# Compression of the cached keys in a hybrid decoder step: three float32r products per weight slice, two row tiles to a PSUM bank in one chunk, and one operand loaded earlier

## The chip, the cores and the metric

The program runs on one core of one Trainium2 chip. The metric is the device time of one launch in microseconds (us), taken as the median over runs. The profiled execution is a separate run with its own time.

## The reference, cut to what matters

One inference step of a two-layer decoder trunk: 512 prompt tokens and 8 sequences of 8 sample tokens. Each layer projects its input with one matrix `w_in` (columns for a convolution, for a sparse attention with compressed, selected and windowed branches, and for a differential attention), mixes, and runs a SwiGLU block. The change touches the compression of keys and values, which runs for "k" and for "v" in each layer, over the 1024 cached positions of 8 sequences and over the 512 prompt positions:

```
def nsa_compress(k, pe, w1, b1, w2):
    B, L, G, D = k.shape
    n16 = L // CMP_STRIDE
    k16 = k[:, :n16 * CMP_STRIDE].reshape(B, n16, CMP_STRIDE, G, D)
    blk = jnp.concatenate([k16[:, :-1], k16[:, 1:]], axis=2) + pe[None, None, :, None, :]
    blk = blk.transpose(0, 1, 3, 2, 4).reshape(B, n16 - 1, G, CMP_LEN * D)
    return jax.nn.gelu(blk @ w1 + b1) @ w2
```

CMP_STRIDE is 16, D is 64, G is 2, so one compressed column is a product over 2048 numbers (16 slices of 128), and neighbouring columns overlap by half.

## The kernel before

One layer runs in stages. `merge` interleaves two generators in program order: `projections` (weight WP) and `compressions` (weight WC); then `prompts` and `samples` (the two attentions); then the output projection with a norm, and the feed-forward block. The tile framework reorders instructions on each engine by its own timeline, so what stands in a queue is read from the built program. Each engine works its queue in order. Loads and stores go through SyncE's queue (SP), gathers of cache pages through GpSimd's (POOL).

**Splitting.** Nearly all dense products are made of float32r halves: `split` writes h = round(x) with ScalarE and l = x - h with VectorE, and `product` adds three matmuls, h·wh, h·wl and l·wh. The 64 sample rows hold h and l side by side in one tile, so for them two matmuls do.

**Chunks.** `chunk` computes 128-token row tiles m = 0..3 and the sample tile m = 4 of a range of columns of `w_in` with `dense_tok`. Its weights stream in eight slices kt. The order of the chunks is d (512 columns), c (280), q (512), e (256); between q and e stand `sample_queries` and `diff_operands`. Five accumulators take the PSUM tags a0, a0, a1, a1, t0. Tag t0 has one buffer, a0, a1 and t1 have two each, h has one. The sinks of the q tiles transpose through t0 as well (line 649, eight groups of four).

**Compression.** `compress` goes over five blocks p: four of two cached sequences, 256 columns (both groups), and one of the prompt, 64 columns. `gather` or `load` brings a page in; `cmp_keys` transposes it through t1 (line 757), and four copies of 64 partitions per bank (line 747 and after, helper line 217) put it into two tiles `kt`. Then 16 plain float32 matmuls with N + 1 columns run over it:

```
for k in range(16):
    aa, jp = k // 4, k % 4
    mm(hid[:, :N + 1], w1[k], kt[jp // 2][:, jp % 2, aa:aa + 2 * N + 1:2], k == 0, k == 15)
```

Their moving columns are every second column of `kt`; the odd last one carries the position embedding. `hid` has the tag h.

**sample_queries** takes an H slot, loads the selection matrix `selp` from the constants, and multiplies it with the gates of the sample rows (`t<-gates,H` in the profile).

Tiles of tags U (30 slots of 1152 words) and H (26 slots of 512 words) are handed out by `W`, the slot freed longest ago first, and returned by `free`; a load into a slot waits for that slot's last reader. Helper lines: 181 load, 184 store, 187 `act`, 190 `tt`, 216 and 217 `cp` (VectorE, ScalarE), 227 `mm`, 350 the transposes of x.

Of the kernel before, what the change touches and what calls it, by code (L numbers as in the profile page):

```python
# [9 lines left out]
F = mybir.dt.float32  # L10
# [38 lines left out]
WC = 120.0  # L49
# [86 lines left out]
def kernel(ctx: ExitStack, tc: tile.TileContext, a: dict, o: dict, nlayers: int = DEPTH):  # L136
# [225 lines left out]
    def product(out, s_, wh, wl, first, last):  # L362


        if not isinstance(s_, tuple):
            mm(out, s_, wh, first, False)
            mm(out, s_, wl, False, last)
        else:
            hs, ls = s_
            mm(out, hs, wh, first, False)  # L370
            mm(out, hs, wl, False, False)
            mm(out, ls, wh, False, last)

    def dense_tok(w_rows, KT, N, st, sink, tail=0, last="h", done=None, raws=None, nh=8):


        acc = [PS(b) for b in ("a0", "a0", "a1", "a1", last)]
# [10 lines left out]
        def step(kt, m, wh, wl):  # L388
            first, last = kt == 0, kt == KT - 1
            out = acc[m][:, :N]  # L390
            product(out, st(kt, m), wh, wl, first, last)
# [20 lines left out]
        for m in (4, 0, 1, 2, 3) if last == "t0" else range(5):  # L412
            for kt, wh, wl, _ in res:
                step(kt, m, wh, wl)
            sink(m, acc[m])
# [39 lines left out]
    def layer(l, x, x_src, raws):  # L455
# [102 lines left out]
        def chunk(c0, N, sink, raws=None):  # L558
            def evac(m, acc):
                z = W("H", [128 if m < 4 else NS, N])  # L560
                if m < 4:
                    cp(z, acc[:, :N])
# [127 lines left out]
        def attention_columns():  # L690
            for c in ORDER:
                if c == "c":
                    new_kv("win")
                if c == "e":
# [25 lines left out]
        def cmp_weights(which):  # L720
            w1s = [W("U", [128, 8, 128]) for _ in range(2)]
            for i in range(2):
                load(w1s[i], a["cmp_w1_" + which][l, i * 1024:(i + 1) * 1024].rearrange("(k p) n -> p k n", p=128))
            w1 = [w1s[k // 8][:, k % 8] for k in range(16)]
# [10 lines left out]
            peT = T("cpe" + which, [128, 2, 2, 4])  # L735
            V.tensor_copy(peT, pt[:, :16].rearrange("p (a q i) -> p q i a", q=2, i=2))
# [3 lines left out]
        def cmp_keys(which, peT, p):  # L740


            n = 128 if p < 4 else 64
            slots = 4 if p < 4 else 2
            kt = [W("U", [128, 2, slots * n + 4]) for _ in range(2)]
            for q in range(2):
                V.tensor_copy(kt[q][:, :, slots * n:], peT[:, q])
            for b2 in range(2 if p < 4 else 1):
                if p < 4:
                    nat = gather("cache_nsa_cmp_" + which, l, 2 * p + b2)  # L750
                else:
                    nat = W("U", [64, 8, 128])
                    load(nat, o["p_cmp_" + which][l, 0].rearrange("(p j) g d -> p j (g d)", j=8))
                for q in range(2):
                    pt = PS("t1").rearrange("p (k t) -> p k t", k=4)
# [879 lines left out]
```

## Time and profile before

| what | value |
|---|---|
| median of 3 runs | 2069.74 us (2063.65 to 2074.16) |
| profiled execution, its own time | 2071.4 us |
| its span (first to last instruction) | 2069.6 us |
| busy share PE / PE weight loads / DVE / ACT / POOL | 93% / 79% / 53% / 44% / 10% |
| mean granted TensorE clock | 0.969 of full speed |

A matmul's duration in the profile includes the time in which it overlaps its neighbours; what a run of matmuls costs is read from start to start. A plain float32 matmul shows as two records of the same shape, a float32r matmul or a float32 transpose as one. The clock column gives 1.00 for 2.4 GHz and 0.50 for 1.2 GHz.

### The profile page before, as it was taken

The numbers are of one execution on the slowest core, as the hardware profiler recorded it, in microseconds if no ns is written. First come the engines' busy times: TensorE is split into PE (matmuls) and PEld (weight loads), VectorE is DVE, ScalarE is ACT, GpSimd is POOL, SyncE is SP. The second block draws the span as 40 slices with busy tenths as digits, with TensorE's granted clock in tenths as the row PEclk, the third lists the DMA queues.
The fourth block names the chain that finished last, engine by engine and source line by source line (L and its number), as shares of the span: only waits on it lengthen the run. The fifth ranks groups of instructions, "written<-read, shape, count | busy, mean of one in ns | idle before, by whom it ended". The sixth has DMA issues, their size and how long they took to land. (4 is left out here: it accounts for less than half of the span.)

```text
span 2069.6 us, 32882 instructions
## 1 busy us (share of the span) xinstructions
PE 1933.5 (93%) x12222; PEld 1631.7 (79%) x12222; DVE 1101.2 (53%) x3012; ACT 916.7 (44%) x2368; POOL 206.7 (10%) x233
## 2 busy tenths in 40 slices
PE   8999888989999999999999997989899999999997
PEld 6887765656689999988879776656566899999885
DVE  3568476866573333323456665678666633333236
ACT  3635565767422333321245545667673223333211
POOL 2011022121010000000120110221110000000002
PEclk9999899999999999999999998999999999999999
DMA  6423143243423332352153321441433332324411
GB/s 200 137 76 103 28 145 128 83 146 99 136 92 117 97 122 83 93 187 77 48 174 108 96 71 45 152 155 57 138 108 118 112 122 82 122 84 130 149 56 51
DMA packets 190252, 223.91 MB, mean 108 GB/s; under 512 B 19092, under 2 KB 138812, under 8 KB 189948
## 3 DMA queue, kind: packets, MB, share of 16 engines
q1 hardware_dynamic: 171660, 154.69, 24.5%
q0 software_dynamic: 18432, 67.12, 10.2%
q8 instruction: 97, 1.59, 0.3%
q14 instruction: 63, 0.52, 0.1%
HBM read 206.23 MB, written 24.15 MB: 111 GB/s over the span
## 5 line engine op out<-in xcount | busy, mean ns | idle before, releaser
L227 PE MATMUL a<-H,U 128*128 128x512 f32 (+3 forms) x2264 | 552.8, 411 | 14.0 <-ACT H L187 11.6
L190 DVE TENSOR_TENSOR H<-H,H 128x512 fp32r<-128x512 f32 (+5 forms) x392 | 255.5, 657 | 510.5 <-ACT H L187 482.8
L227 PEld LDWEIGHTS a<-H,U 128*128 128x128 f32 (+1 forms) x2264 | 386.2, 190 | 111.2 <-issue 15.4
L187 ACT ACTIVATE H<-H 128x512 fp32r<-128x512 f32 (+4 forms) x418 | 240.8, 583 | 519.9 <-DMA H<-in_ffn_w_dram 298.8
L227 PE MATMUL a<-U,H 128*128 128x288 f32 (+2 forms) x3008 | 399.2, 306 | 7.9 <-DMA U<-in_cache_diff_v_dram,idx 6.7
L227 PEld LDWEIGHTS a<-U,H 128*128 128x128 f32 (+1 forms) x3008 | 370.2, 181 | 21.7 <-DMA U<-in_cache_diff_v_dram,idx 7.3
L227 PE MATMUL t<-U,H 128*128 128x288 f32 x1584 | 288.7, 297 | 0.4 <-ACT U L187 0.4
L227 PEld LDWEIGHTS t<-U,H 128*128 128x128 f32 x1584 | 243.5, 190 | 1.0 <-ACT U L187 0.6
L227 PE MATMUL a<-U,U 128*128 128x512 f32 (+4 forms) x744 | 200.7, 379 | 7.9 <-ACT H L187 3.7
L227 PE MATMUL h<-U,U 128*128 128x257 f32 (+5 forms) x708 | 152.4, 376 | 13.1 <-ACT U L217 13.0
L217 ACT ACTIVATE U<-t 64x256 f32<-64x256 f32 (+4 forms) x393 | 142.8, 366 | 45.6 <-PE t L757 24.5
L227 PEld LDWEIGHTS a<-U,U 128*128 128x128 f32 x744 | 129.4, 191 | 34.2 <-ACT U L187 7.4
L227 PEld LDWEIGHTS h<-U,U 128*128 128x128 f32 (+1 forms) x708 | 114.6, 185 | 40.3 <-ACT U L217 17.3
L227 PE MATMUL h<-U,H 128*128 128x288 f32 x528 | 140.9, 296 | 0.0
L187 ACT ACTIVATE U<-H 128x288 fp32r<-128x288 f32 (+4 forms) x160 | 64.4, 438 | 143.8 <-DVE H L190 104.1
L217 ACT ACTIVATE H<-t 128x512 f32<-128x512 f32 (+1 forms) x172 | 94.9, 564 | 45.6 <-PE t L1145 23.5
L547 DVE SCALAR_TENSOR_TENSOR U<-U,cw,U 128x512 f32<-128x512 f32 x240 | 109.4, 510 | 0.1
L227 PEld LDWEIGHTS h<-U,H 128*128 128x128 f32 x528 | 99.3, 188 | 0.0
L190 POOL TENSOR_TENSOR U<-U,U 128x512 f32<-128x512 f32 x24 | 33.6, 1417 | 599.1 <-DVE rs_u L321 459.9
L187 ACT ACTIVATE U<-t 128x256 fp32r<-128x256 f32 (+4 forms) x132 | 47.1, 370 | 97.0 <-PE t L350 40.8
L190 DVE TENSOR_TENSOR U<-H,U 128x64 fp32r<-128x64 f32 (+6 forms) x204 | 69.9, 385 | 31.1 <-ACT U L187 24.8
L216 DVE COPY H<-t 128x512 f32<-128x512 f32 (+1 forms) x92 | 57.2, 626 | 45.7 <-PE t L1214 15.6
(293 smaller groups left out, 2268.9 us busy)
## 6 DMA issues: line engine op xcount, KB each, us to landing
H<-in_ffn_w_dram SPq DMA_DIRECT2D x264, 256.0 KB
H<-in_w_in_dram SPq DMA_DIRECT2D x64, 256.0 KB
H<-in_w_out_dram SPq DMA_DIRECT2D x32, 256.0 KB
xd<-U SPq DMA_DIRECT2D x24, 256.0 KB
U<-xd SPq DMA_DIRECT2D x12, 512.0 KB
U<-in_x_prompt_dram SPq DMA_DIRECT2D x8, 512.0 KB
H<-in_state_nsa_win_v_dram SPq DMA_DIRECT2D x16, 256.0 KB
H<-in_state_nsa_win_k_dram SPq DMA_DIRECT2D x16, 256.0 KB
```

Source lines behind the costliest of these rows:

```text
L187: S.activation(out, in_, func, **kw)
L190: return (eng or V).tensor_tensor(out, x, y, op=op)
L216: return V.tensor_copy(out, in_)
L217: return S.activation(out, in_, AF.Copy)
L227: return PE.matmul(out, lhsT, rhs, start=start, stop=stop)
L547: V.scalar_tensor_tensor(out=ac, in0=ex, scalar=wc, in1=ac, op0=OP.mult, op1=OP.add)
```

## The change

In the compression, `cmp_weights` splits w1 into wh and wl (two U tiles each), and the position embedding into halves as well. `compress` first copies a page with ScalarE into two H tiles `halves` (four copies of 256 elements per partition), which puts the two groups side by side, and frees the page. `cmp_keys` then works for one half q: it transposes four 128-wide pieces, and one `split` per bank writes the h and l tiles of `kt` with rows of equal parity (r) contiguous. The 16 slices, now eight per half q, have three float32r matmuls each on contiguous columns: 256 of them (258 in the first block, 64 in the prompt's). The embedding's columns, two VectorE copies per block before, come by four small GpSimd copies per block.

In `dense_tok`, a chunk with 2N <= 512 (only chunk e, N = 256) puts two row tiles into one bank: a0, a0 and a1 in place of five banks; the first matmul of the second tile of a bank waits for that of the first one, and the copy out waits for both tiles.

`selp` is loaded before chunk q, not in `sample_queries`. WC goes from 120 to 128.

```diff
-        acc = [PS(b) for b in ("a0", "a0", "a1", "a1", last)]
+        if 2 * N > 512:
+            acc = [PS(b) for b in ("a0", "a0", "a1", "a1", last)]
+        else:
+            acc = [t[:, c * 256:(c + 1) * 256] for t in (PS(b) for b in ("a0", "a0", "a1")) for c in range(2)]
...
+                if c == "q":
+                    own["selp"] = W("H", [64, 512])
+                    load(own["selp"], a["cst"][:64, CST["selp"][0]:CST["selp"][0] + 512])
...
+                raw = W("U", [128, 8, 128])
+                load(raw, a["cmp_w1_" + which][l, i * 1024:(i + 1) * 1024].rearrange("(k p) n -> p k n", p=128))
+                wh, wl = (W("U", [128, 8, 128], FR) for _ in range(2))
+                split(wh, wl, raw)
...
-                for q in range(2):
-                    pt = PS("t1").rearrange("p (k t) -> p k t", k=4)
-                    for j in range(4):
-                        PE.transpose(pt[:, j, :n], nat[:, 4 * q + j], ident[:n, :n])
-                    for g in range(2):
-                        c0 = (b2 * 2 + g) * n
-                        for par in range(2):
-                            cp(kt[q][par * 64:(par + 1) * 64, :, c0:c0 + n], pt[g * 64:(g + 1) * 64, par::2, :n])
...
+            kt = [W("U", [128, 2, 2, len(nats) * n + 3], FR) for _ in range(2)]
+            for part in range(2):
+                G.tensor_copy(kt[part][:, :, :, len(nats) * n:], peT[:, part, q].bitcast(F))
+            for b2, nat in enumerate(nats):
+                pt = PS("t1")
+                for i in range(4):
+                    PE.transpose(pt[:, i * n:(i + 1) * n], nat[q][:, i * 128:(i + 1) * 128], ident[:n, :n])
+                split(*(t[:, :, :, b2 * n:(b2 + 1) * n] for t in kt), pt[:, :2 * w].rearrange("p (i c r) -> p i r c", i=2, r=2))
...
+                    for q in range(2):
+                        for g in range(2):
+                            act(halves[q][:, :, g], nat[:, 4 * q:4 * q + 4, g * 64:(g + 1) * 64].rearrange("p (i k) d -> p i k d", k=2))
...
+                            mm(hid[:, :M], wh, kh, first, False)
+                            mm(hid[:, :M], wh, kl, False, False)
+                            mm(hid[:, :M], wl, kh, False, last)
```

**The first block on PE.** The names are out<-moving,stationary; h is the accumulator, U tiles are `kt` and w1, first holds the identity, a and t with U and H are the chunk. Layer 0, block p = 0 of "k", before and then now:

```order
L227 MATMUL a_70_257<-H_111_482,U_31_125 128x512
L227 MATMUL a_70_257<-U_114_488,U_27_121 128x512
L227 MATMUL h_375<-U_87_331,U_76_279 128x257 x2
L757 MATMUL t_109_464<-first_63,U_108_462 128x128
L227 MATMUL h_375<-U_88_332,U_76_279 128x257 x2
```

```order
L227 MATMUL t_73_260<-H_109_451,U_32_126 128x512
L781 MATMUL t_106_424<-first_63,H_91_328 128x128 x4
L227 MATMUL h_359<-U_98_360,U_77_281 128x258
L227 MATMUL h_359<-U_99_361,U_77_281 128x258
L227 MATMUL h_359<-U_98_360,U_78_282 128x258
```

Each slice has three matmuls where it had one, and the transposes read copies in H tiles, not the gathered page.

**PE behind chunk q.** Layer 0; a with U_27 is the tail of chunk q, 128x256 is chunk e, lines 649 and 668 are the transposes of the q tiles, 1068, 1078, 1110 and 1120 those of `sample_queries`, 866 (910 now) those of `diff_operands`. Before and then now:

```order
L227 MATMUL a_378_2046<-U_421_2295,U_31_125 128x512
L227 MATMUL t_461_2474<-c_242_1310,H_410_2251 64x64 x4
L649 MATMUL t_437_2344<-first_63,H_434_2337 128x128 x4
L227 MATMUL t_464_2483<-gates_237,H_465_2484 128x24 x4
L1068 MATMUL t_467_2498<-first_63,H_424_2307 128x64 x4
L649 MATMUL t_438_2353<-first_63,H_429_2331 128x128 x4
L1068 MATMUL t_468_2507<-first_63,H_425_2308 128x64 x4
L1078 MATMUL t_469_2516<-first_63,H_268_1449 128x64 x4
L649 MATMUL t_443_2379<-first_63,H_440_2372 128x128 x4
L227 MATMUL t_470_2527<-c_242_1310,H_459_2467 32x64 x2
L227 MATMUL a_479_2566<-H_484_2571,U_24_118 128x256
```

```order
L227 MATMUL a_451_2501<-U_491_2755,U_31_125 128x512
L227 MATMUL t_530_2912<-gates_237,H_447_2496 128x24 x4
L668 MATMUL t_506_2799<-first_63,H_503_2792 128x128 x4
L227 MATMUL a_543_2986<-H_546_2989,U_24_118 128x256
L227 MATMUL a_544_2987<-H_546_2989,U_24_118 128x256
L227 MATMUL a_545_2988<-H_546_2989,U_32_126 128x256
L1110 MATMUL t_532_2925<-first_63,H_494_2767 128x64 x4
L1110 MATMUL t_533_2934<-first_63,H_495_2768 128x64 x4
L1120 MATMUL t_534_2943<-first_63,H_315_1739 128x64 x4
L227 MATMUL a_543_2986<-H_547_2990,U_24_118 128x256
```

The last products of the compression (`c` tiles) have left this place for one ahead of q's end, chunk e begins two entries behind the gates, and its sample tile goes to an a bank with the first slice, where it was the last to run in t0.

**SP around chunk e's loads.** in_cst with 64x512 is `selp`, in_w_in with 128x256 are slices of chunk e, cbv and c are vectors and weights of the next layer's compression. Before, then the two pieces of now:

```order
L181 DMA H_409_2233<-in_w_in_dram 128x512
L181 DMA H_495_2633<-in_w_in_dram 128x256
L181 DMA cbv_11966<-in_cmp_b_v_dram 128x1
L181 DMA H_465_2484<-in_cst_dram 64x512
L181 DMA H_486_2573<-in_w_in_dram 128x256
L181 DMA H_489_2593<-in_w_in_dram 128x256
L181 DMA H_504_2693<-in_w_in_dram 128x256
L181 DMA c_2229_10927<-in_cmp_w_k_dram 128x64 x2
L181 DMA H_506_2698<-in_w_in_dram 128x256
```

```order
L184 DMA out_p_win_v_dram<-H_431_2398 128x128
L181 DMA H_447_2496<-in_cst_dram 64x512
L184 DMA out_p_win_k_dram<-H_415_2307 128x128
L184 DMA out_s_win_k_dram<-H_403_2267 8x8x128
L184 DMA out_p_win_v_dram<-H_437_2441 128x128
L184 DMA out_p_win_k_dram<-H_426_2357 128x128
L181 DMA H_477_2658<-in_w_in_dram 128x512
```

```order
L181 DMA H_483_2704<-in_w_in_dram 128x512
L181 DMA cbv_12512<-in_cmp_b_v_dram 128x1
L181 DMA c_2295_11353<-in_cmp_w_k_dram 128x64 x2
L181 DMA H_548_2991<-in_w_in_dram 128x256
L181 DMA H_551_3011<-in_w_in_dram 128x256
L181 DMA H_563_3091<-in_w_in_dram 128x256
```

`selp` now stands ahead of all slices of chunk q, and chunk e's slices still stand behind the two loads for the next layer.

## Rows read from the trace of the kernel before

**Rows 1.** The page, busy time and share of the span.

```profile
PE 1933.5 (93%) x12222; PEld 1631.7 (79%) x12222; DVE 1101.2 (53%) x3012; ACT 916.7 (44%) x2368; POOL 206.7 (10%) x233
```

**Rows 2.** Windows: length, busy us of PE, PEld, DVE, ACT, POOL, clock, DMA.

```profile
40.00:240.00 200.00, 190.95 (x1081) 163.35 (x1080) 120.60 (x332) 103.40 (x278) 26.09 (x27) 0.99 0.32 92
240.00:282.00 42.00, 31.87 (x195) 29.09 (x196) 23.01 (x63) 21.14 (x58) 3.87 (x5) 0.72 0.28 74
...
1264.00:1306.00 42.00, 31.22 (x189) 28.68 (x190) 22.32 (x61) 21.86 (x56) 3.44 (x4) 0.72 0.25 70
```

**Rows 3.** Groups of PE by line, tiles and shape.

```profile
L227 PE MATMUL a<-U,H 128*128 128x288 f32 x2496 | 346.1, 298 | 0.0
...
L227 PE MATMUL h<-U,U 128*128 128x257 f32 x512 | 126.5, 395 | 10.2 <-ACT U L217 10.1
...
L227 PE MATMUL h<-U,U 128*128 128x65 f32 x128 | 15.2, 270 | 0.0
```

**Rows 4.** Timeline of PE, four places: start, us, operation, count.

```profile
44.68 6.52 PE L227 MATMUL h<-U,U 128*128 128x257 f32 x28
51.05 0.93 PE L757 MATMUL t<-first,U 128*128 128x128 f32 x7
...
224.76 1.50 PE L227 MATMUL h<-U,U 128*128 128x65 f32 x12
226.07 1.18 PE L227 MATMUL a<-H,U 128*128 128x512 f32 x4
...
278.90 0.52 PE L227 MATMUL a<-H,U 128*128 128x256 f32 x3
...
281.75 0.60 PE L866 MATMUL t<-first,U 128*128 128x128 f32 x4
```

**Rows 5.** Waits of PE from 0 to 290 us: total, times, longest.

```profile
PE t L227 <- DMA H<-in_cst_dram: 8.3, 2, 4.6
PE h L227 <- ACT U L217: 4.8, 3, 2.2
...
PE t L757 <- ACT U L217: 2.6, 3, 1.2
```

**Rows 6.** Timeline of PE behind chunk q, both layers; idle time and its end in brackets.

```profile
239.91 0.66 PE L649 MATMUL t<-first,H 128*128 128x128 f32 x4
245.12 1.90 PE L227 MATMUL t<-gates,H 64*128 64x24 f32 x8 [4.55 <-DMA H<-in_cst_dram]
...
268.01 1.22 PE L227 MATMUL a<-H,U 128*128 128x256 f32 x4 [2.55 <-ACT H L187]
269.03 1.05 PE L649 MATMUL t<-first,H 128*128 128x128 f32 x4
...
1268.57 1.90 PE L227 MATMUL t<-gates,H 64*128 64x24 f32 x8 [4.59 <-DMA H<-in_cst_dram]
```

**Rows 7.** Windows inside that stretch, columns as in rows 2.

```profile
243.00:257.00 14.00, 11.01 (x55) 9.83 (x56) 9.51 (x25) 9.31 (x26) 0.26 (x1) 0.52 0.20 52
...
264.00:274.00 10.00, 7.43 (x34) 7.07 (x35) 2.70 (x7) 2.84 (x7) 0.00 (x0) 0.50 0.37 103
```

**Rows 8.** Timeline of SP's queue.

```profile
241.42 0.33 SPq L181 DMA_DIRECT2D cbv<-in_cmp_b_v_dram  x1
242.52 0.53 SPq L181 DMA_DIRECT2D H<-in_cst_dram  x1
...
252.97 12.53 SPq L181 DMA_DIRECT2D H<-in_w_in_dram  x3
```

**Rows 9.** Groups of DVE and ACT by shape, from 0 to 290 us.

```profile
L658 DVE SCALAR_TENSOR_TENSOR U<-t,U 64x512 fp32r<-64x512 f32 x8 | 5.5, 688 | 2.4 <-ACT U L187 2.2
...
L217 ACT ACTIVATE U<-t 64x256 f32<-64x256 f32 x127 | 48.1, 379 | 13.3 <-PE t L757 11.6
...
L187 ACT ACTIVATE U<-t 64x512 fp32r<-64x512 f32 x8 | 4.7, 591 | 1.8 <-PE t L649 1.2 <-DVE U L658 0.3
...
L187 ACT ACTIVATE H<-H 128x256 fp32r<-128x256 f32 x7 | 2.9, 415 | 4.1 <-DMA H<-in_w_in_dram 4.1
```

More of the change, by code (lines that the diff above doesn't have):

```diff
@@ L388, in step @@
         def step(kt, m, wh, wl):
-            first, last = kt == 0, kt == KT - 1
+            first, last = kt == 0 and (2 * N > 512 or m % 2 == 0), kt == KT - 1 and (2 * N > 512 or m in (1, 3, 4))
             out = acc[m][:, :N]
-            product(out, st(kt, m), wh, wl, first, last)
+            i, j = product(out, st(kt, m), wh, wl, first, last)
+            if 2 * N <= 512 and kt == 0:
+                if m % 2:
+                    wait_for(i, starts[m - 1])
+                starts[m] = i
+            return j
         for kt in range(KT - tail):
@@ L720, in cmp_weights @@
         def cmp_weights(which):
-            w1s = [W("U", [128, 8, 128]) for _ in range(2)]
+            w1s = [[], []]
             for i in range(2):
-                load(w1s[i], a["cmp_w1_" + which][l, i * 1024:(i + 1) * 1024].rearrange("(k p) n -> p k n", p=128))
-            w1 = [w1s[k // 8][:, k % 8] for k in range(16)]
+                raw = W("U", [128, 8, 128])
+                load(raw, a["cmp_w1_" + which][l, i * 1024:(i + 1) * 1024].rearrange("(k p) n -> p k n", p=128))
+                wh, wl = (W("U", [128, 8, 128], FR) for _ in range(2))
+                split(wh, wl, raw)
+                free(raw)
+                w1s[0].append(wh)
+                w1s[1].append(wl)
+            w1 = [(w1s[0][k // 8][:, k % 8], w1s[1][k // 8][:, k % 8]) for k in range(16)]
             w2p = T("c2", [128, 192])
@@ L734, in cmp_weights @@
             PE.transpose(pt[:, :16], pe, ident[:16, :16])
-            peT = T("cpe" + which, [128, 2, 2, 4])
-            V.tensor_copy(peT, pt[:, :16].rearrange("p (a q i) -> p q i a", q=2, i=2))
+            peT = T("cpe" + which, [128, 2, 2, 2, 2, 3], FR)
+            G.memset(peT.rearrange("p a q i r c -> p (a q i r c)").bitcast(F), 0.0)
+            for q in range(2):
+                split(peT[:, 0, q, :, :, :2], peT[:, 1, q, :, :, :2], pt[:, :16].rearrange("p (c r q i) -> p q i r c", c=2, r=2, q=2)[:, q])
@@ L737, in cmp_weights @@
             free(pe)
             return w1s, w1, w2p, b1, peT
[L740 to L745, printed above, removed]
-            for q in range(2):
[L747 to L754, printed above, removed]
-                    pt = PS("t1").rearrange("p (k t) -> p k t", k=4)
-                    for j in range(4):
-                        PE.transpose(pt[:, j, :n], nat[:, 4 * q + j], ident[:n, :n])
-                    for g in range(2):
-                        c0 = (b2 * 2 + g) * n
-                        for par in range(2):
-                            cp(kt[q][par * 64:(par + 1) * 64, :, c0:c0 + n], pt[g * 64:(g + 1) * 64, par::2, :n])
-                    yield 0.5
-                free(nat)
@@ L822, in compress @@
             cmp_out(which, w2p, *held)
-            free(*w1s)
+            free(*w1s[0], *w1s[1])
         def compressions():
@@ L1052, in sample_queries @@
             pg = PS("t1")
-            selp = W("H", [64, 512])
-            so = CST["selp"][0]
-            load(selp, a["cst"][:64, so:so + 512])
+            selp = own.pop("selp")
             for p in range(4):
```

61 lines of the change are left out of this document (45 added, 16 removed).

## The prediction

> **What bounds the kernel now.** The page comes first: PE is busy 93% of the span, DVE 53%, ACT 44% [rows 1]. So PE's own work counts at nearly full price, and beside it only the places where PE stands still or runs slowly. The windows show where that is near the change. From 40 to 240 us (projections and compression of layer 0) PE is busy 190.95 of 200 us; the stretch behind chunk q, 240 to 282 us, has 31.87 of 42 us at a mean clock of 0.72, and layer 1 repeats it at 1264 to 1306 us with 31.22 [rows 2]. The waits of PE up to 290 us name the causes: 4.6 us in one piece for a load from the constants, which is `selp`, and 4.8 and 2.6 us for ACT's copies that feed the compression [rows 5]. The profiled execution took 2071.4 us for a span of 2069.6 us, 1.7 us above the median of the runs (2069.74 us); sums are made against 2071.4 us.
>
> **Products, whole blocks.** The pace of the old ones is read from start to start: 28 records from 44.68 us, and the next operation starts at 51.05 us, which is 0.2275 us each; a product is two records, 0.455 us [rows 4]. All 512 records are 256 products [rows 3]: 16 slices, 4 blocks, k and v, two layers. The new ones are float32r with 256 or 258 moving columns and 128 stationary ones. The trace has that shape in chunk e: 24 matmuls from 278.90 us to 281.75 us at full clock, 0.119 us each [rows 4]. Three make 0.357 us, 0.098 us less than 0.455. Over 256 products that is **-25.1 us**. Bounds: the 65-column records run at 0.109 us (next term), so three cannot be taken below 0.327 us (-32.8 us); 288 columns cost 346.1 / 2496 = 0.139 us [rows 3], so 0.417 us at most (-9.7 us). I take 0.119 us, the same shape and type.
>
> **Products, the prompt's block.** 128 records of 65 columns are 64 products [rows 3]. Twelve records from 224.76 us to 226.07 us give 0.109 us each [rows 4], far above what 65 columns should take next to 257 at 0.2275 us: here loading the stationary tile sets the pace. It is the same tile for 64 float32r columns, so two records become three matmuls at 0.109 us: 64 x 0.109 = **+7.0 us**. Lower bound: at a quarter of the 256-column pace three cost 0.09 us (-8 us); upper bound: the 256-column pace itself, three at 0.119 us (+8.9 us). I take 0.109 us since the weight tile doesn't change. The Trainium skill, page "TensorE: Matmul & The Clock Gate", section "Back-to-back issue gap", gives about 81 ns for a weight load and matmul of 128 columns in a stream; by that figure, as an estimate from the page, this term would be +1.6 us, and no row here shows such a pace for a 128-column float32 weight tile.
>
> **The feed of the compression.** Transposes stay equal in number. Per layer ACT loses 128 copies of 64x256 (0.379 us) and 16 half as wide (half of 0.379 to 0.379; I take 0.27), 52.8 us. It gains 72 copies of 128x256 (0.415 us), 36 halves of a split (0.591 us, four of them half as wide) and four 1024-wide w1 splits (twice 0.591 us): 29.9 + 20.1 + 4.7 = 54.7 us [rows 9]. So ACT stays level. DVE gains 36 second halves (0.688 us, four narrower) and four for w1 at twice that: some 29 us per layer, less 20 tiny copies [rows 9]. DVE was busy 120.60 of 200 us there [rows 2], so it goes to about 147: no bound, but its queue now stands between transposes and product, which it did not. Behind a waiting subtraction on DVE stand convolution taps and weight splits; PE waits for the latter. Against that, a bank is emptied by one ACT operation and one DVE operation (0.591 + 0.688 us) in place of four copies in a row (1.52 us), and the page copies run ahead of the transposes. Bounds: if the waits named L217 go, 7.4 us in layer 0 and I count the same in layer 1, -14.8 us; if one subtraction of 0.688 us shows at each of 40 half blocks (5 blocks, 2 halves, k and v, 2 layers), +27.5 us. I take **+4 us**, nearer to hidden, since the scheduler has chunk matmuls to put between. The GpSimd copies stand ahead of gathers in POOL's queue, which was busy 26.09 of 200 us [rows 2]; nothing for them.
>
> **Behind chunk q.** Three edits meet here. `selp` now stands in SP's queue ahead of chunk q's slices, so its load has some 20 us more; the waits of 4.55 and 4.59 us at the gates go [rows 6]. In the old queue it was issued at 242.52 us, behind a vector for the next layer at 241.42 us [rows 8]. What is late next is the t0 chain: eight transpose groups of the q tiles, from 239.91 us to 269.03 us [rows 6], each of a q tile's rotated ones with ACT 0.591 and DVE 0.688 us behind it before t0 is free [rows 9]. Chunk e's sample accumulator needed t0 after all of them, so its weight tiles were held and the later slices waited for H slots: SP took 12.53 us over three issues [rows 8] and PE waited 2.55 us for a weight split [rows 6]. Now the sample tile is in an a1 bank, and chunk e's matmuls fill PE between the groups. I count three pieces per layer. The wait, 4.6 us. The slow clock behind it: from 243 to 257 us PE had 11.01 us of work at 0.52 [rows 7], which at full clock is about 5.7 us, so 5.3 us. The second wait, 2.5 us. That is 12.4 us; I keep 12, and leave the second slow stretch (7.43 us of work at 0.50 [rows 7], worth 3.7 us) to the t0 chain, which stays. Twice 12 is **-24 us**. Bounds per layer: 2.5 us (DVE's rotations still hold the second group back, so half of the first wait only moves) and 16.1 us (all of 12.4 and 3.7): -5 to -32 us. The wait between two first matmuls of a bank and the shared copies out are hidden by the e matmuls of other slices; uncovered they would cost one copy, 0.4 us per bank. WC only shifts the interleaving; nothing for it.
>
> **The sum.** 2071.4 - 25.1 + 7.0 + 4 - 24 = 2033.3, so **2033 us**.
>
> **The rivals.**
> *The chain stays.* Behind chunk q only the 2.5 us per layer of the lower bound come, because the q tiles' rotations on DVE (9.51 of 14 us busy [rows 7]) hold back whatever PE could do. Time: 2033.3 + 24 - 5 = 2052 us. For it: DVE is the fuller engine in that window. Against: chunk e needs neither the rotations nor t0 now.
> *The feed shows* (the other side). Each half block starts with ACT 0.591 and DVE 0.688 us after its transposes, 1.28 us, and each block with four page copies, 1.66 us. If all of it stands open, 40 x 1.28 + 20 x 1.66 = 84 us, against the +4 taken: 2113 us. It decides from about 46 / 40 = 1.15 us per half block, where the gains of 18.1, 24 and the 4 us are used up. For it: DVE had no part in this path before. Against: PE's waits for the old, longer copies were 7.4 us in a layer [rows 5].
> *The clock stays low behind q.* If that stretch, which holds many transposes, ran at 0.52 anyway, the 5.3 us are not won: 2033.3 + 2 x 4.9 = 2043 us. For it: the clock fell while PE stood still and stayed low through 11.01 us of mixed work [rows 7]. Against: the seven transposes at 51.05 us, behind 6 us of products, took 0.93 us [rows 4]. The Trainium skill, same page, "Part 4: PE-mode transpose", says transposes don't count as PE-busy for the clock; by that rule this rival would hold, and the trace doesn't separate it from the standstill.
> *Later stages give it back.* The attentions start earlier with another alternation of copies between ACT and DVE. A third of the gain lost is 2046 us.
>
> **How the numbers follow.** Forecast 0.60 (its own range 2015 to 2048 us, from the bounds of one term at a time), chain stays 0.16, feed shows 0.08, clock low 0.10, later stages 0.06. Below 2012 us I put 0.06, with the lower bounds of the products and of q's stretch together; above 2058 us 0.13, nearly all from the feed and a part of the chain rival. So 2012 to 2058 us. A measurement of this kernel can tell about 0.5% (10 us) from no change: faster is below 2059 us. From the cases: faster 0.85, same 0.08, slower 0.07.
>
> **What would show it.** After: 258 and 256 columns at 0.119 us from start to start and 64 columns at 0.109; no wait for in_cst at the gates; PE's clock at or near 1.00 behind chunk q until the t0 chain bites; the stretch from q's last matmul to the first scores near 30 us in place of 42; PE's waits ahead of h below 10 us per layer. Wrong it would be if PE waited for a DVE subtraction ahead of most half blocks, if float32r matmuls of 64 columns cost several times 0.109 us, or if the stretch behind q kept its 42 us.

## The result, and the profile after

| kernel | median | runs | ratio to before, 95% interval |
|---|---|---|---|
| before | 2067.61 us (2057.23 to 2074.16) | 8 | |
| changed | 2086.85 us (2083.99 to 2097.28) | 8 | 1.011 (1.009 to 1.013) |

The change made the kernel 1.1% slower; 2033 us were forecast. The profiled execution took 2084.94 us, its span 2083.2 us, the mean granted clock was 0.965. First the page of the changed kernel, the answer to [rows 1]:

```profile
PE 1924.4 (92%) x12542; PEld 1644.7 (79%) x12542; DVE 1145.7 (55%) x3053; ACT 902.3 (43%) x2315; POOL 236.1 (11%) x317
```

PE has 9.1 us less busy time in a span that is 13.6 us longer. The windows of PE, answers to [rows 2] (from 40 to 240 us) and, with the stretch from the gates to the first scores, for layer 0 and layer 1:

```profile
40.00:240.00 200.00, 183.20 (x1196) 166.87 (x1195) 135.85 (x345) 91.33 (x240) 39.11 (x57) 0.94 0.32 92
...
249.80:293.40 43.60, 30.04 (x195) 27.13 (x194) 22.73 (x62) 18.71 (x49) 3.90 (x5) 0.77 0.24 65
1279.60:1321.60 42.00, 29.15 (x195) 26.52 (x194) 22.77 (x62) 20.01 (x50) 3.89 (x5) 0.80 0.26 70
```

In the projections PE is busy 183.20 of 200 us where it was 190.95, and the clock is 0.94 where it was 0.99. Less work did not make the stretch shorter: it turned into idle time and slow time. Here are PE's waits from 0 to 290 us, the answer to [rows 5]:

```profile
PE a L227 <- ACT H L187: 11.8, 5, 4.0
PE t L227 <- DMA H<-in_cst_dram: 4.0, 1, 4.0
PE t L668 <- DVE U L677: 3.3, 1, 3.3
PE h L227 <- ACT U L187: 2.8, 3, 1.5
...
PE t L781 <- ACT kbd L187: 2.3, 1, 2.3
PE h L227 <- ACT H L187: 1.9, 1, 1.9
PE t L781 <- DVE U L190: 1.8, 1, 1.8
```

The remaining 4.0 us for in_cst are at the start of the program; the wait at the gates is gone. In its place stand waits for the q tiles' rotations (L668 <- DVE U), for the new feed (the rows with h and L781) and, longest of all, for weight splits (a <- ACT H), which before were

```profile
PE a L227 <- ACT H L187: 4.7, 5, 2.5
```

**A ledger for every trace below.** From the records of one profiled execution three sums are made over a stretch: PE's busy time at the granted clock, so that a microsecond at 0.50 counts half (*work*); the other half of such microseconds (*slow clock*); and the time in which no matmul record runs (*idle*). Together they are the length. The stretches are the *projections* (up to the first gates matmul, in layer 0 from the start of the span, in layer 1 from the last two matmuls of layer 0's feed-forward with h as accumulator) and *behind the gates* (from there to the first scores), both layers summed. Each trace is one execution, and executions of one kernel lie up to 13 us from their median, so a line says where time went, and the medians say how much. The two spans below are 13.6 us apart, the medians 19.2 us.

| us | projections: length = work + slow + idle | behind the gates: length = work + slow + idle |
|---|---|---|
| before | 479.4 = 436.8 + 5.1 + 37.5 | 75.0 = 44.3 + 18.9 + 11.8 |
| changed | 488.4 = 417.6 + 23.9 + 47.0 | 85.6 = 46.7 + 12.4 + 26.4 |

Over the whole span, work fell by 17.5 us, slow clock rose by 8.4 us and idle time by 22.7 us.

### The profile page after: what moved, and what is told of

The parts are those of the page before. It is cut to its first block, busy times and chain, and to the rows that moved or that the text cites. A ratio compares the mean times of both kernels' runs of the same rounds, so it can differ in the third digit from the quotient of the medians.

```text
span 2083.2 us, 33674 instructions
## 1 busy us (share of the span) xinstructions
PE 1924.4 (92%) x12542; PEld 1644.7 (79%) x12542; DVE 1145.7 (55%) x3053; ACT 902.3 (43%) x2315; POOL 236.1 (11%) x317
## 3 DMA queue, kind: packets, MB, share of 16 engines
q0 software_dynamic: 18432, 67.12, 10.2%
## 5 line engine op out<-in xcount | busy, mean ns | idle before, releaser
L227 PEld LDWEIGHTS a<-H,U 128*128 128x128 f32 (+1 forms) x2292 | 391.7, 191 | 139.5 <-ACT H L187 37.8
L187 ACT ACTIVATE H<-H 128x512 fp32r<-128x512 f32 (+5 forms) x418 | 241.1, 583 | 516.7 <-DMA H<-in_ffn_w_dram 300.5
L227 PE MATMUL h<-U,U 128*128 128x256 f32 (+4 forms) x1028 | 151.2, 310 | 15.8 <-ACT U L187 5.9
L227 PEld LDWEIGHTS h<-U,U 128*128 128x128 f32 (+1 forms) x1028 | 136.1, 202 | 27.8 <-ACT U L187 7.4
L187 ACT ACTIVATE U<-t 128x256 fp32r<-128x256 f32 (+5 forms) x204 | 86.9, 441 | 138.1 <-PE t L781 43.0
L190 DVE TENSOR_TENSOR U<-t,U 128x512 fp32r<-128x512 f32 (+3 forms) x196 | 87.5, 454 | 61.7 <-ACT U L187 41.9
L190 DVE TENSOR_TENSOR U<-H,U 128x64 fp32r<-128x64 f32 (+6 forms) x204 | 69.8, 384 | 38.1 <-ACT U L187 31.7
```

Of the source, the lines that this page charges most:

```text
L187: S.activation(out, in_, func, **kw)
L190: return (eng or V).tensor_tensor(out, x, y, op=op)
L227: return PE.matmul(out, lhsT, rhs, start=start, stop=stop)
```

## The experiments

Ratios are to the kernel before, run beside each kernel on the same chip, with the 95% interval. "Compression alone" is the changed kernel with chunk e in five banks, `selp` loaded in `sample_queries` and WC = 120 as before; most experiments build on it.

### The parts apart: compression alone, the edits at q, the load of selp, WC

The edit of the first run, against the changed kernel:

```diff
-WC = 128.0
+WC = 120.0
-        if 2 * N > 512:
+        if N > 0:
...
-                    own["selp"] = W("H", [64, 512])
-                    load(own["selp"], ...)
```

> The compression's new form alone: chunk e in five banks, selp loaded in sample_queries and WC 120, as before. Feed theory (the products give their 18 us, but what feeds them, the page copies, splits and H slots, makes PE wait for chunk weights and costs some 35 to 40 us): 2080 to 2095 us, the time of the changed kernel or slower, and the windows from 40 to 240 us lose about 10 us of PE's busy time per layer as in the changed kernel. Clash theory (each part is good by itself, together they run out of H slots): 2045 to 2060 us. Pacing theory (WC 128 spoils the interleaving): 2050 to 2070 us.

> The old compression and WC 120, with two row tiles to a bank in chunk e and selp loaded ahead of chunk q. As forecast (12 us per layer behind chunk q): 2044 us. Feed theory, in which only the new compression's traffic spoils the stretch behind q: 2044 to 2058 us, with the wait for in_cst at the gates gone and the stretch from q's end to the first scores at 31 to 37 us. Chain theory (the q tiles' transposes and rotations set the end whatever PE has to do): 2062 to 2068 us, the stretch keeps 41 to 43 us.

> The kernel before with selp loaded ahead of chunk q and nothing else. If the wait of 4.6 us per layer at the gates is worth its length: 2058 us, and with the half clock behind it 2048 us. If another wait takes its place (weights of chunk e that come late, or the t0 chain): 2065 to 2069 us, and the gates start some 4.5 us earlier while the first scores do not.

> The changed kernel with WC back at 120. Pacing theory: at least half of the loss goes, 2060 to 2075 us. Feed theory and clash theory: 2080 to 2094 us, within 0.4% of the changed kernel, with the same kind of waits on PE.

| run | median | ratio | projections | behind the gates |
|---|---|---|---|---|
| compression alone | 2081.16 us | 1.0061 (1.0034 to 1.0087) | 493.2 = 418.9 + 28.4 + 45.8 | 77.2 = 43.4 + 17.2 + 16.6 |
| both edits at q alone | 2083.84 us | 1.0066 (1.0043 to 1.0090) | 480.5 = 437.6 + 6.2 + 36.6 | 77.3 = 46.3 + 11.0 + 20.0 |
| selp alone | 2078.84 us | 1.0044 (1.0021 to 1.0067) | 481.8 = 435.2 + 12.0 + 34.6 | 80.6 = 46.0 + 12.8 + 21.8 |
| changed, WC 120 | 2090.85 us | 1.0095 (1.0071 to 1.0120) | 484.6 = 420.5 + 23.2 + 40.9 | 85.1 = 45.8 + 14.3 + 24.9 |

Each part alone makes the kernel slower, and their losses (0.6% and 0.7%) add up to about that of the whole, so the parts do not clash with each other; and WC is not the cause. The clash theory and the pacing theory fall. The compression alone has the saved work (-17.9 us in the projections) and the loss (+23.3 us slow clock, +8.3 us idle).

The edits at q gain little where they were made, 7.4 us of the 24 forecast, and in the changed kernel almost none of that is left. From the start of chunk q's last matmul to the first scores before took 43.3 us in layer 0 and 44.0 us in layer 1; with both edits 41.6 and 38.3, with `selp` alone 42.2 and 40.9, in the changed kernel 43.9 and 42.3. PE's timeline with `selp` alone shows what came in the place of the wait:

```profile
246.30 1.07 PE L227 MATMUL t<-gates,H 64*128 64x24 f32 x8
...
249.61 0.43 PE L1088 MATMUL t<-first,H 64*128 64x64 f32 x4 [1.31 <-ACT U L217]
251.31 0.69 PE L1098 MATMUL t<-first,H 64*128 64x64 f32 x4 [1.27 <-ACT U L217]
254.39 1.12 PE L668 MATMUL t<-first,H 128*128 128x128 f32 x4 [2.39 <-DVE U L677]
...
272.80 1.22 PE L227 MATMUL a<-H,U 128*128 128x256 f32 x4 [2.97 <-ACT H L187]
```

The gates run without a wait, but no earlier (246.3 us against 245.1 before, as the compression's last products now stand just ahead of them, the last one at 243.3 us in place of 227.4). Then PE waits for the copies of `sample_queries` (1.31 and 1.27 us), for the q tiles' rotations on DVE (2.39 us) and for a weight split of chunk e (2.97 us). As far as the two timelines tell, the 4.6 us had covered these.

With both edits at q alone the attention of layer 0, from the first scores to the last, takes 250.5 us in place of 240.8. That is as much as the two spans differ by (2078.9 against 2069.6 us). Its matmuls stand in another order there, and the next run asks what order can do.

### Another order, and nothing else

```diff
-WC = 120.0
+WC = 128.0
```

> The kernel before with WC at 128: no operation is added or taken away, only the order in which two streams are interleaved. It measures what another order alone does. If order matters little: within 3 us of before. If each new order costs some waits that the old one does not have (the order of before being a good one among many): 2075 to 2085 us, as in the runs with chunk q's edits alone.

2071.56 us, 1.0021 (1.0005 to 1.0037). This order alone costs 0.2%. But the order of an attention stage matters when it switches: in the traces of this study PE's matmuls there either stand nearly as before (33 stages, 237.6 to 245.1 us, among them all those of before and of the changed kernel) or in a clearly other order. The second kind is layer 0 with both edits at q (250.5 us), layer 1 of the widened run below (251.0), layer 1 with the taps over 56 units (244.7), both layers with half the taps (251.0 and 249.4), and both with NH = 2 (246.9 and 236.7). The change itself doesn't switch it, so this is no part of its loss, but it blurs the medians of the runs that do.

### Does the prompt's block lower the clock by itself?

PE's timeline of the compression alone, and the windows around the clock's fall (columns as in [rows 2]):

```profile
120.18 7.34 PE L227 MATMUL h<-U,U 128*128 128x64 f32 x47
127.33 1.20 PE L227 MATMUL t<-H,c 128*128 128x128 f32 x4
```

```profile
116.40:123.20 6.80, 6.80 (x46) 6.11 (x44) 4.10 (x10) 0.25 (x1) 2.58 (x2) 1.00 0.39 118
123.20:130.00 6.80, 6.80 (x29) 6.45 (x29) 6.39 (x15) 2.37 (x9) 3.31 (x3) 0.50 0.42 117
```

PE stands still for no moment in either window, and yet the clock is halved from the second on, in the middle of 47 matmuls of 64 columns. The test streams the 64 columns four times over:

```diff
+                            M_ = M
+                            if p == 4:
+                                M_ = 256
+                                kh, kl = (t.unsqueeze(1).to_broadcast([128, 4, 64]) for t in (kh, kl))
```

> The compression's new form alone (as in the run of it alone, 2081 us), but the 192 matmuls of the prompt's blocks stream their 64 columns four times over, 256 columns each; only the first 64 are used. In that run's trace the clock falls to half in two stretches of layer 0 (6.8 and 10.2 us) in which trains of 47 such matmuls run with no idle time ahead. Narrow-column theory (short matmuls back to back lower the clock, at no idle time): each costs 0.119 in place of 0.112 us, +1.3 us, and the half-clock stretches at the trains go, worth 12 to 17 us: 2066 to 2071 us. Standstill theory (only PE's idle time lowers the clock): 2082 to 2084 us, the half-clock stretches stay.

2086.21 us, 1.0087 (1.0057 to 1.0118): slower as a whole, where 2066 to 2071 us were forecast. Layer 1's attention switched its order (+10.8 us), which is most of the miss but not all of it. At the place itself the trace shows what the narrow-column theory said:

```profile
120.72 5.93 PE L227 MATMUL h<-U,U 128*128 128x256 f32 x47
126.49 0.61 PE L227 MATMUL t<-H,c 128*128 128x128 f32 x4
```

```profile
117.40:126.40 9.00, 9.00 (x63) 8.40 (x62) 5.73 (x13) 0.63 (x1) 2.77 (x2) 1.00 0.34 107
223.40:232.90 9.50, 9.40 (x62) 8.57 (x63) 3.26 (x6) 2.69 (x5) 0.00 (x0) 1.00 0.11 43
```

Four times the columns take 5.77 us from start to start for 47 matmuls in place of 7.15 us, because the clock stays at 1.00. In the projections of this trace slow clock is 14.7 us, against 28.4 us. But work and idle time are longer (425.6 against 418.9 and 48.0 against 45.8 us), so the projections are only 4.8 us shorter (488.4 against 493.2). The count over all traces says the same: of the 32 trains of 48 narrow float32r matmuls in eight traces (four to a trace), 25 have half clock within them or in the 3.5 us behind them, 22 of these with no idle time in the train or shortly ahead of it; of 12 widened trains in three traces none; of 24 trains in six traces of the old form (32 records of 65 columns, plain float32) one, and that one had 2.6 us of idle time in or just ahead of it. (The old trains are shorter, 32 records, and of another type; length and type were not tried apart.) The Trainium skill, page "TensorE: Matmul & The Clock Gate", section "HAM oscillation — how this bites in real kernels", puts a slow clock down to DMA waits and advises, for a thin operand, to pad it or to do all its K tiles before the next wait. These rows show another case: the clock fell with no wait, and more columns kept it up with no wait taken away.

### Less work: the prompt's columns beside others

The prompt's 64 columns join the 256 of the last pair of sequences, so that 192 matmuls have 320 columns and none has 64.

```diff
-            for p in range(5):
+            for p in range(4):
...
+            kv = [[W("U", [128, 2, L + 3], FR) for _ in range(2)] for _ in range(2)]
```

> The compression's new form alone, with the prompt's 64 columns put beside the 256 of the last pair of sequences: no matmuls of 64 columns, 192 of 320 columns in place of 192 of 256 and 192 of 64. Two more U tiles for that block. Narrow-column theory: 16.4 us of matmuls less (192 x 0.112 less 192 x 64 / 2400) and 12 to 17 us of slow clock less: 2048 to 2054 us. Standstill theory: the matmuls alone, 2064 to 2066 us. Slot theory (the feed is short of U and H tiles): the two more U tiles bring new waits, 2068 us or more.

> The changed kernel (2086.9 us) with the prompt's 64 columns beside the 256 of the last pair of sequences. Narrow-column theory: 2056 to 2062 us. Standstill theory: 2070 us. Slot theory: 2073 us or more.

2080.10 us, 1.0064 (1.0042 to 1.0087), on the compression alone, and 2104.08 us, 1.0181 (1.0153 to 1.0210), on the changed kernel. The first has 13.5 us less work in the projections than the compression alone (405.4 against 418.9 us) and 17.9 us more idle time (63.7 against 45.8), and its median is only 1.1 us lower. So PE's work no longer sets the length of this stage. (In the trace of the second, more of the chunks' work falls behind the gates, 81.6 us where the changed kernel has 46.7; why it loses that much was not tried.) Its waits from 20 to 250 us name the feed:

```profile
PE h L227 <- ACT U L187: 6.9, 4, 4.0
PE t L787 <- DVE U L190: 6.3, 3, 3.7
PE t L227 <- DVE H L871: 4.2, 1, 4.2
```

These are the split's two halves (ACT, then DVE) ahead of products and of the next transposes, and the gelu chain. The slot theory had the number right, but runs below (no page copies, NH 2) speak against it.

### What PE waits for: VectorE, the page copies, the U tiles, GpSimd

DVE's load in three slices of layer 0, first before, then the compression alone:

```profile
100.00:120.00 20.00, 20.00 (x118) 17.23 (x117) 15.26 (x37) 8.56 (x26) 2.26 (x2) 1.00 0.30 87
140.00:160.00 20.00, 18.77 (x97) 15.07 (x96) 16.39 (x54) 14.72 (x37) 5.82 (x2) 1.00 0.37 89
180.00:200.00 20.00, 17.79 (x97) 14.52 (x95) 17.89 (x58) 13.04 (x39) 5.97 (x4) 1.00 0.40 109
```

```profile
100.00:120.00 20.00, 20.00 (x124) 17.32 (x123) 20.00 (x47) 7.03 (x14) 4.78 (x3) 1.00 0.21 50
140.00:160.00 20.00, 12.05 (x73) 10.49 (x72) 19.39 (x55) 9.10 (x20) 3.48 (x5) 0.93 0.37 100
180.00:200.00 20.00, 18.99 (x143) 17.30 (x141) 19.45 (x63) 13.03 (x38) 8.45 (x12) 1.00 0.36 96
```

In these slices DVE (the third figure after the length) was at 15.3 to 17.9 of 20 us before and is full or nearly so now, and PE falls to 12.05 us in the second. A full slice alone doesn't stop PE: from 100 to 120 us it is busy throughout, and before had DVE at 18.37 us from 160 to 180 us with PE at 20.00. The longest waits of the projections are those of a chunk's matmuls for their weight split. From 20 us to the gates of layer 0 the kernel before has none of 0.3 us or more; the compression alone has

```profile
PE a L227 <- ACT H L187: 7.7, 2, 4.9
```

The longer one ends at 158.40 us. By the trace's semaphores PE waits there for ACT's half of the split, ACT for a load that was issued at 155.72 us, and the load for its slot, which a DVE operation read until 155.69 us. So DVE's queue can reach PE by way of a slot and a load, and not only by the subtraction ahead of a product. The taps of the convolution are the largest block of work there. They are spread more thinly (first three runs), or every second one is left out (the next two):

```diff
-TC = 36.0
+TC = 56.0
```

```diff
-                for w in range(CW):
+                for w in range(0, CW, 2):
...
-            yield from beside(attention_columns(), TC, conv_taps(), 62.0)
+            yield from beside(attention_columns(), TC, conv_taps(), 32.0)
```

> The compression's new form alone (2081 us), with the convolution's taps on DVE spread over 56 in place of 36 units of chunk cost: no operation added or taken away. In its trace DVE is busy 20.0 of the 20 us from 100 to 120, 19.4 from 140 to 160 and 19.5 from 180 to 200. DVE theory (the subtractions of the split queue behind taps and rotations there, and PE behind them): no slice of 20 us from 100 to 200 us above 18.5, PE's idle time in the projections (25.1 us in layer 0, 20.7 in layer 1) falls by 4 to 10 us per layer and the slow clock with it, 2060 to 2070 us. Page-copy theory (ACT's four copies of each page and the H tiles they hold make PE wait): 2076 to 2086 us, the waits stay.

> The kernel before with the taps spread over 56 units, the control for the run above. DVE theory: before had no subtraction between transposes and products, so little moves: within 5 us of before. If the taps were in the way before too: 2058 to 2062 us, and the gain of the run above is not the compression's.

> The compression's new form with the prompt's 64 columns beside 256 others (2080 us, 31 us less of PE's work than before and 33 us more idle time) and the taps spread over 56 units. DVE theory: the work that merging saves shows once DVE has room, 2045 to 2060 us. Page-copy theory: 2074 to 2085 us.

> The kernel before with every second of the 31 taps of the convolution left out, spread over the same length of the chunks: some 25 us of DVE work per layer less. It is the control for the next run. VectorE theory: 2058 to 2067 us, since little waited for DVE before. U-tile and GpSimd theories say nothing else here.

> The compression's new form alone (1.0061 of before) with the same taps left out. VectorE theory: with DVE's load of the projections back at or below that of before, the 18 us of the products show against the control: 2040 to 2052 us. U-tile and GpSimd theories: the loss stays, 8 to 14 us above the control.

| run | median | ratio | projections |
|---|---|---|---|
| compression alone, TC 56 | 2079.93 us | 1.0066 (1.0048 to 1.0085) | 482.7 = 422.5 + 18.1 + 42.1 |
| before, TC 56 | 2066.57 us | 0.9998 (0.9984 to 1.0012) | 476.6 = 438.2 + 3.4 + 35.0 |
| compression with merged columns, TC 56 | 2071.69 us | 1.0024 (1.0010 to 1.0038) | 478.0 = 407.8 + 15.8 + 54.3 |
| before, half the taps | 2063.09 us | 0.9966 (0.9950 to 0.9981) | 477.5 = 434.8 + 11.1 + 31.7 |
| compression alone, half the taps | 2088.72 us | 1.0089 (1.0069 to 1.0110) | 480.3 = 422.2 + 23.3 + 34.8 |

Spreading the taps gives the compression alone nothing that can be measured (DVE is still at 20.00 us from 160 to 180 us of its trace), and 0.4% where the merged columns have taken more work off PE. With half the taps PE's idle time in the projections falls by 11.0 us (45.8 to 34.8), twice as much as in the old form (37.5 to 31.7): DVE's queue is a part of the new idle time. Most of that is at the weight splits: PE's waits for them (a <- ACT H, both layers, from 20 us on) are 0.9 us before, 12.6 with the compression alone and 2.4 with half the taps. But the time does not fall, for the slow clock stays (23.3 us; all four narrow trains have half clock) and both attentions switched their order, which in the traces is 16.2 of the 25.0 us to the control. So VectorE alone is not shown to be the cause. Nor was it wholly relieved: from 140 to 160 us DVE still has 19.47 us with half the taps, where the control has 15.55.

Three runs take away one other suspect each: the four page copies on ACT with their H tiles (the page then stays in its U tile for longer); the U tile for a chunk's last weights; the small copies on GpSimd.

```diff
-                            act(halves[q][:, :, g], nat[...])
+                    nats.append([nat[:, 4 * q:4 * q + 4].rearrange("p j d -> p (j d)") for q in range(2)])
```

```diff
-NH = 1
+NH = 2
```

```diff
-                G.tensor_copy(kt[part][:, :, :, len(nats) * n:], peT[:, part, q].bitcast(F))
+                V.tensor_copy(kt[part][:, :, :, len(nats) * n:], peT[:, part, q].bitcast(F))
```

> The compression's new form alone, without the four ACT copies of each page and without the H tiles for them: the transposes take 128 contiguous numbers of the page (both groups of one position) in place of two positions of one group, so the regrouping of the page is left out. 72 ACT copies of 0.42 us per layer and four H tiles per block less, PE and DVE as before that. Page-copy theory: PE's waits for ACT H (12.1 us up to 320 us in the changed kernel) mostly go and the time falls to 2058 to 2068 us. DVE theory: 2074 to 2082 us, DVE stays at 19 of 20 us in the slices from 100 to 200 us.

> The compression's new form alone, with the halves of the last weight slice of each chunk in two H tiles in place of one U tile (NH 2 in place of 1). About 24 of the 30 U tiles are held during the projections, some 22 before. U-tile theory (kt's and the pages' tiles wait for a slot that PE still reads as weights, as at 145.73 us of the run of the compression alone): 2062 to 2072 us, and no wait of a GpSimd copy for PE's a product. VectorE theory and GpSimd theory: 2076 to 2084 us.

> The compression's new form alone, with the 40 small copies per layer of the embedding's columns on VectorE, as before, in place of GpSimd, so that gathers stand behind no copy. GpSimd theory (a copy that waits for its tile holds up the gathers behind it, and ACT's page copies with them): 2062 to 2072 us. VectorE theory: 2080 to 2088 us, as 40 operations of 0.1 us or so are added to its queue. U-tile theory: 2077 to 2083 us, the same tiles are waited for.

| run | median | ratio | projections |
|---|---|---|---|
| no page copies | 2078.22 us | 1.0050 (1.0033 to 1.0068) | 483.8 = 420.8 + 21.5 + 41.5 |
| NH 2 | 2096.03 us | 1.0125 (1.0103 to 1.0147) | 491.4 = 418.2 + 26.2 + 47.0 |
| small copies on VectorE | 2078.68 us | 1.0055 (1.0035 to 1.0075) | 489.0 = 423.1 + 22.3 + 43.6 |

None takes the loss away. The U-tile and GpSimd theories fall (with NH 2 the waits of GpSimd copies for a chunk's matmuls are gone in layer 0, and yet this run is the slowest of the three; both its attentions switched their order); the page copies are worth 4.3 us of idle time in one trace, and nothing that the medians can tell.

### Both halves of the cause together

These two versions keep the attentions in the order of before: widened trains with the taps over 56 units, and widened trains with half the taps (TC 32, where the control has 36).

> The compression's new form alone, the prompt's matmuls widened to 256 columns and the taps spread over 56 units; the attentions keep the order of before. Nothing of the reference's result is left out. Two-cause theory: the slow clock at the narrow trains goes (12 us) and VectorE is partly relieved: 2060 to 2068 us, at or just below before. If a third cause holds most of the loss: 2074 us or more.

> Both causes taken away at once: the compression's new form alone, the prompt's matmuls widened to 256 columns, every second tap of the convolution left out (32 units, so that the attentions keep the order of before). The control is the kernel before with the same taps left out, 2063 us (0.9966 of before). Two-cause theory: the products' 18 us less 1 to 6 us of rest show against the control: 2045 to 2052 us, 0.988 to 0.992 of before. A third cause: 2058 us or more, 0.995 of before or more.

| run | median | ratio | projections |
|---|---|---|---|
| widened, TC 56 | 2071.20 us | 1.0003 (0.9985 to 1.0021) | 484.0 = 424.8 + 16.0 + 43.3 |
| widened, half the taps | 2061.72 us | 0.9949 (0.9929 to 0.9969) | 468.9 = 422.6 + 10.7 + 35.6 |

The first is a whole version of the kernel with nothing left out: the loss of the compression (0.6%) is gone, and nothing is gained over before; the time lies between the two ranges forecast. How much of this the trains' clock makes is not shown: the run with the taps alone spread (1.0066) has projections of the same length (482.7 against 484.0 us) and one attention in another order. The second has to be held against its control, before with half the taps. Its projections are 8.6 us shorter (468.9 against 477.5): 12.2 us less work, slow clock the same (10.7 against 11.1), idle time 3.9 us longer. But the control's trace is the longest of its twelve executions, 8.7 us above their median, so the 8.6 us can be that alone. By the medians it is 0.9949 against 0.9966, which is 3.5 us and within both intervals: that the saved work shows with both causes taken away is not shown. The forecast of 2045 to 2052 us for this run was too low, and the bound that it gave for a third cause, 2058 us, is passed.

What may be left is seen at the start of `compress` for v, in the slice from 140 to 160 us that stayed full. There the compression alone, half the taps, NH 2, the small copies on VectorE and these two runs each have a wait of PE for DVE of 2.3 to 3.7 us in layer 0; here in the last run (its line 778 is line 781 of the changed kernel):

```profile
144.95 0.63 PE L778 MATMUL t<-first,H 128*128 128x128 f32 x4 [0.78 <-ACT H L187]
145.58 0.36 PE L227 MATMUL h<-U,U 128*128 128x258 f32 x1
148.48 1.84 PE L227 MATMUL h<-U,U 128*128 128x258 f32 x7 [2.55 <-DVE U L190]
```

The product of the second half block waits 2.55 us, while DVE works through rotations of chunk d. That it is the rest of the loss was not tried.

## Why the prediction was wrong

Three steps failed: the gain behind chunk q (24 us forecast, 1.1 measured), the feed (+4 us, against 28.9 of idle time and slow clock) and the prompt's block (its clock stood at nothing, and lost 8.5 us). The work saved on the products came as forecast.

**The products were right, as work.** "PE's own work counts": 18.1 us less were forecast, the ledger has 17.5 us over the whole span. The groups, the answer to [rows 3], and the paces, the answer to [rows 4]:

```profile
L227 PE MATMUL h<-U,U 128*128 128x256 f32 x576 | 86.8, 303 | 12.1 <-ACT U L187 5.3 <-ACT H L187 4.3 <-DVE U L190 2.5
...
L227 PE MATMUL h<-U,U 128*128 128x258 f32 x192 | 26.2, 287 | 0.1
L227 PE MATMUL h<-U,U 128*128 128x64 f32 x192 | 25.7, 292 | 0.7 <-ACT U L187 0.5 <-DVE U L190 0.2
```

```profile
117.05 5.44 PE L227 MATMUL h<-U,U 128*128 128x64 f32 x48
122.33 0.30 PE L540 MATMUL t<-first,H 128*64 128x128 f32 x1
...
144.88 2.91 PE L227 MATMUL h<-U,U 128*128 128x258 f32 x23
147.62 1.04 PE L781 MATMUL t<-first,H 128*128 128x128 f32 x8
```

64 columns: 5.28 us for 48, 0.110 us each (0.109 forecast). 258 columns: 2.74 us for 23, 0.119 us (0.119).

**The prompt's block had a price that no term held.** The step "two records become three matmuls at 0.109 us" took the pace of the old records over, and with it their clock. In the changed kernel two of the four trains have half clock at them, 10.2 and 6.8 us long, which is 8.5 us lost (the first had 0.7 us of idle time in and ahead of it, the second none); in the compression alone three, 11.9 us.

**The feed was mis-sized.** +4 us was taken, from bounds of -14.8 to +27.5. The projections of the changed kernel have 9.5 us more idle time, although the two waits at the gates (9.1 us, which the ledger counts there) are gone: 18.6 us. The slow clock of the waits comes on top: of 18.8 us more, 8.5 us are the trains', and 10.3 us lie elsewhere: the other five half-clock stretches of layer 0 each have 1.6 to 3.7 us of idle time just ahead of them. The term had no line for that, though the one behind q had. Together 28.9 us, just past the dear bound. The path was wrong too: both bounds were made of waits at the compression's own transposes and products, but the largest part of the new idle time is waits for the chunks' weight splits. From 20 us on, over both layers, these went from 0.9 to 13.1 us, those at the compression's own only from 17.2 to 19.1. The prediction named these ("weight splits; PE waits for the latter") and gave them no price. Its sign for the feed, waits ahead of h below 10 us per layer, was met (6.0 us in layer 0) and missed this. The reason given, that DVE's share "goes to about 147: no bound", was an average over 200 us. In the three slices of 20 us above DVE was at 15.3 to 17.9 us before, and the change filled them: 20.00 us in this one of the changed kernel.

```profile
140.00:160.00 20.00, 18.10 (x115) 15.99 (x114) 20.00 (x54) 7.88 (x17) 0.77 (x3) 1.00 0.15 38
```

**Behind chunk q the rival "the chain stays" came nearest.** 24 us were forecast, 5 us by the rival. The stretch from q's last matmul to the first scores went from 43.3 and 44.0 us to 43.9 and 42.3, 1.1 us in all. PE's timeline there, the answer to [rows 6]:

```profile
249.83 1.07 PE L227 MATMUL t<-gates,H 64*128 64x24 f32 x8
...
255.53 1.01 PE L227 MATMUL a<-H,U 128*128 128x256 f32 x3 [4.04 <-ACT H L187]
...
276.40 0.85 PE L668 MATMUL t<-first,H 128*128 128x128 f32 x4 [3.34 <-DVE U L677]
...
281.68 1.01 PE L227 MATMUL a<-H,U 128*128 128x256 f32 x3 [2.56 <-ACT H L187]
```

The wait at the gates is gone as foreseen, and chunk e's first weight split is late by 4.04 us, its last by 2.56 us, and the q tiles' rotations by 3.34 us. The prediction named the t0 chain as late next, but counted on chunk e's matmuls to fill PE; chunk e's weights came too late to do it, and 41 of its matmuls ran in one piece after the last group of the chain. The rival had the length, but only half of the cause: it named the rotations (3.34 us), and the two waits for weights are 6.60 us. The half clock behind the gates did get less (18.9 to 12.4 us for both layers), the idle time grew by more (11.8 to 26.4).

**The rivals.** "The feed shows" was right in direction; its 1.28 us at each half block are not what the trace has (layer 0 has ten waits for the feed at its 20 half blocks, of 2.3 us at most). "The clock stays low behind q" held in part: the mean rose to 0.77 and 0.80, from 0.72 in the nearest windows of before [rows 2], but from 249.83 to 264.00 us it was 0.64, where the prediction expected it at or near 1.00. The rest of the program gave 6.0 us back.

**What stays open.** That the narrow trains lose clock without a wait, and that widening them keeps it, is shown; that fewer taps on DVE shorten PE's idle time is seen in one trace of each kernel. How much of the compression's loss each makes is not shown in the medians: with both away, 3.5 us remain of 12.2 us of saved work, within both intervals, so a third cause is not ruled out. Of the changed kernel's loss behind the gates the waits are named, not each tried.

## What to carry to other kernels

A stretch in which PE is nearly full can still be paced by its feed: before counting saved matmul time as gain, look at the feeding engines in slices of some 20 us, since an average over 200 us hides the slices that are nearly full, and follow a wait back through slot and load to the engine that held the slot. Count a wait that an edit removes only after asking what was hidden under it: here other waits of 1.3 to 4.0 us were. When a product is split into more and narrower matmuls, look at the granted clock at and behind them; here four times the columns, in a widened operand, kept it up.

## What the runs showed of the hardware

Float32r matmuls of 64 columns back to back, at 0.110 us each, went with half clock (1.2 GHz), in the train or just behind it, in 25 of 32 trains, in 22 of them with no idle time; the same trains with 256 columns in none of 12, at about 0.12 us each. A moving operand that repeats its 64 columns four times by a stride of zero ran at that pace. Plain float32 trains of 65 columns, at 0.109 us a record and 32 records long where the others have 48, kept the full clock in 23 of 24.
